# Thirteen quads of block products with seven multiplications in two projections, six shared load buffers, and a later transposition

## The chip, the cores and the metric

The kernel runs on one core of a Trainium2 chip. The metric is device time in microseconds from the start to the end of one execution. TensorE (PE) multiplies matrices: an operand of 128 x 128 is loaded into the array (PEld in the profile) and up to 512 columns run past it; sums go to PSUM, eight banks of 128 x 512 float32. VectorE (DVE) and ScalarE (ACT) work element by element, SyncE (SP) issues most of the DMAs, and GpSimd (POOL) issues some. Each engine carries out its instructions in order.

## The reference

Two layers over 256 positions of width 2048, in float32. The lines that matter here are the two output projections and what stands around them:

```python
# layer A
h = rms_norm(x, a_norm[layer])
q, k, v, g = jnp.split(h @ a_w_in[layer], 4, axis=-1)
o = chunked_relbias_attention(split_heads(q), split_heads(k), split_heads(v), a_rel_bias[layer]).reshape(b, s, D_INNER)
x = x + (o * jax.nn.silu(g)) @ a_w_out[layer]          # projection "ao": 4096 -> 2048
# shared keys and values, forget gates from x; then layer B
q, g = jnp.split(rms_norm(x, b_norm[lb]) @ b_w_in[lb], 2, axis=-1)
o = forgetting_attention(split_heads(q), k_sh, v_sh, cum_logf_h).reshape(b, s, D_INNER)
x = x + (o * jax.nn.silu(g)) @ b_w_out[lb]             # projection "bo": 4096 -> 2048
return rms_norm(x, final_norm)
```

## The kernel before

Every product is a sum of three: each float32 operand is split into a high part `hi` (rounded by ACT) and the rest `lo` (subtracted by DVE), both in the format fp32r, and the products hi·hi, hi·lo and lo·hi are added up in PSUM (`mm3`).

The 256 positions are two tiles, t = 0 and 1. A projection makes four units of 512 columns: `ao0` to `ao3` for layer A, `bo0` to `bo3` for layer B. Each unit has a PSUM bank for each t (`acc`), and its 4096 rows of weights come in 16 sub-blocks, each of two blocks of 128 rows (KB = 2). A sub-block is one load of 512 KB into a buffer `raw`, one split into `hi` (ACT) and `lo` (DVE), and 2 blocks x 2 tiles x 3 = 12 matmuls of 512 columns. `Feed` keeps the loads and splits ahead of the matmuls: `raw` has RAW = 3 buffers, in one ring for all weights of the kernel, `hi` and `lo` have SPLIT = 4 each, and DEPTH = 3 sub-blocks stand ready. A load is issued by SP when the oldest buffer has been read by both splits; SP takes them in program order.

`project` walks through the sub-blocks in the order of a list, unit by unit, and calls two functions: `begun`, which after the unit's twelfth sub-block loads the residual `xin` (in the one buffer "R"), and `closed`, after its last. `ao_closed` adds the two banks to `xin`, writes it to the scratch `x1d`, and starts the turn of the new x, which layer B needs with the width on partitions: for units 0 to 2 that is `x1_to_T`: a STREAM_TRANSPOSE by DVE from `xin` into the one buffer `xinY`, 16 DMAs by POOL from there to `xinZ`, and then splits into `x1Th` and `x1Tl`, in steps some sub-blocks apart (`[8, 1, 1, 1]`). For the last unit it is `x_to_T`, eight transposes on PE ("xT<-ident,xin") at once. Layer B starts with `bqg0`, whose twelve-matmul sub-blocks take their x from these.

`bo_closed` adds the residual, squares it (ACT) and scales it by the last gain; when `bo3` closes, `finish_tile` ends each t with the norm and the output. The last eight sub-blocks of `bo3` (LATE = 8) do t = 0 at once and t = 1 at the end, so that t = 0 can be finished beside the matmuls of t = 1; five of them keep their splits in own tiles (`keep`).

## Time and profile before

| | |
|---|---|
| time, median of 3 runs | 1760.83 us (1760.07 to 1763.58) |
| the profiled execution | 1762.27 us, its span 1760.4 |
| PE busy | 1746.0 us, 99% of the span |
| DVE busy | 1159.1 us, 66% |
| ACT busy | 1084.1 us, 62% |
| POOL busy | 515.7 us, 29% |
| layer A's inputs and attention | 0 to about 711 us |
| projection `ao` | about 711 to 879 us |
| layer B's inputs and attention | about 879 to 1582 us |
| projection `bo` | about 1582 to 1752 us |

The span is the time between the first and last instruction that the profiler saw; the execution's own time is a little longer. A row of the profile names line, engine and operation, the tile that is written and after the arrow those that are read. "Idle before" is the time in which the engine had nothing to do ahead of such an instruction, and after the arrow stands what ended it. Rows of the chain of waits have the start, the duration and the work that the end of the kernel waited for.

### The profile page before, as it was taken

What the parts mean: (1) busy time and instruction counts of PE and PEld (TensorE: products, weight loads), DVE (VectorE), ACT (ScalarE), POOL (GpSimd) and SP (SyncE); (2) the same over time, 40 slices, a digit from 0 to 9 for tenths busy, and PEclk for the clock granted to TensorE, in tenths of its full rate; (3) what the DMA queues carried; (4) which work ended last, traced back from release to release, by engine and by line L of the source; (5) the groups of instructions that cost most, each with busy time, mean ns of one, the idle gap of its engine ahead of it and who ended that gap; (6) DMA issues with size and microseconds to landing.
All of it is one profiled execution on the core that took longest, in us unless ns stands there. A gap on an engine that the chain in (4) does not pass through costs nothing.

```text
span 1760.4 us, 25526 instructions
## 1 busy us (share of the span) xinstructions
PE 1746.0 (99%) x8387; PEld 1533.1 (87%) x8387; DVE 1159.1 (66%) x1662; ACT 1084.1 (62%) x2063; POOL 515.7 (29%) x1071
## 2 busy tenths in 40 slices
PE   9999999999999999999999999999999999999997
PEld 7888888888888888888888888888888888888886
DVE  6666666666666666655666777777777777776654
ACT  6555555555555555555556777777777777765443
POOL 1333333333333333111104333333333333333000
PEclk9999999999999999999999999999999999999999
DMA  7867776777777777777766777777777777776665
GB/s 255 248 218 227 225 225 224 225 224 224 223 224 224 224 225 222 222 239 240 239 195 226 236 227 222 227 224 226 223 228 226 227 222 231 249 225 222 216 217 161
DMA packets 143652, 396.34 MB, mean 225 GB/s; under 512 B 31104, under 2 KB 38560, under 8 KB 143392
## 3 DMA queue, kind: packets, MB, share of 16 engines
q1 hardware_dynamic: 107472, 354.25, 63.8%
q0 software_dynamic: 32256, 37.29, 6.6%
q10 hardware_dynamic: 3792, 3.17, 0.6%
q8 instruction: 66, 1.08, 0.2%
q14 instruction: 66, 0.54, 0.1%
HBM read 351.05 MB, written 4.23 MB: 202 GB/s over the span
## 4 chain that ended last, share of the span: by engine, by line
PE 94%; DMA 2%; DVE 2%; ACT 1%; issue 0%; POOL 0%; SPq 0%; ACTq 0%; DVEq 0%; POOLq 0%
PE bkv_acc L182 19%; PE bqg_acc L182 19%; PE avg_acc L182 18%; PE aqk_acc L182 17%; PE ao_acc L182 9%; PE bo_acc L182 8%; DMA bo_raw<-in_b_w_out 1%; PE op L448 1%; PE s0p L414 1%; PE op L391 0%; PE s1p L390 0%; PE s1p L391 0%; PE op L392 0%; PE op L390 0%; PE s1p L392 0%
## 5 line engine op out<-in xcount | busy, mean ns | idle before, releaser
L363 POOL DMA_DIRECT2D sgZ<-sgY x512 | 250.9, 497 | 194.6 <-DVE sgY L360 96.5
L363 POOL DMA_DIRECT2D turned<-turned x448 | 219.9, 498 | 267.7 <-PE avg_acc L182 93.0
L233 DVE SCALAR_TENSOR_TENSOR bqg_lo<-bqg_raw,gain,bqg_hi 128x512 fp32r<-128x512 f32 x256 | 182.0, 747 | 97.1 <-ACT bqg_hi L232 97.0
L232 ACT ACTIVATE bqg_hi<-bqg_raw,gain 128x512 fp32r<-128x512 f32 x256 | 170.9, 714 | 114.1 <-PE bqg_acc L182 50.2
L238 DVE TENSOR_TENSOR avg_lo<-avg_raw,avg_hi 128x1024 fp32r<-128x1024 f32 x127 | 153.4, 1219 | 115.6 <-ACT avg_hi L237 115.5
L238 DVE TENSOR_TENSOR aqk_lo<-aqk_raw,aqk_hi 128x1024 fp32r<-128x1024 f32 x125 | 152.4, 1219 | 92.7 <-ACT aqk_hi L237 92.6
L233 DVE SCALAR_TENSOR_TENSOR bkv_lo<-bkv_raw,gain,bkv_hi 128x512 fp32r<-128x512 f32 x256 | 181.3, 748 | 45.3 <-ACT bkv_hi L232 42.3
L237 ACT ACTIVATE avg_hi<-avg_raw 128x1024 fp32r<-128x1024 f32 x127 | 132.5, 1055 | 124.5 <-PE aqk_acc L182 60.1
L182 PE MATMUL bqg_acc<-bqg_hi,x1Th 128*128 128x512 f32 x512 | 191.6, 384 | 0.0
L182 PE MATMUL aqk_acc<-aqk_hi,xTh 128*128 128x512 f32 x512 | 190.9, 383 | 0.2
L182 PE MATMUL aqk_acc<-aqk_lo,xTh 128*128 128x512 f32 x512 | 189.0, 379 | 1.2 <-DVE aqk_lo L238 1.2
L182 PE MATMUL avg_acc<-avg_hi,xTh 128*128 128x512 f32 x512 | 190.2, 382 | 0.0
L182 PE MATMUL avg_acc<-avg_lo,xTh 128*128 128x512 f32 x512 | 188.9, 379 | 0.3 <-DVE avg_lo L238 0.3
L182 PE MATMUL bqg_acc<-bqg_hi,x1Tl 128*128 128x512 f32 x512 | 189.1, 379 | 0.0
L182 PE MATMUL bkv_acc<-bkv_hi,x1Th 128*128 128x512 f32 x512 | 189.0, 379 | 0.0
L182 PE MATMUL aqk_acc<-aqk_hi,xTl 128*128 128x512 f32 x512 | 188.9, 379 | 0.0
L182 PE MATMUL avg_acc<-avg_hi,xTl 128*128 128x512 f32 x512 | 188.8, 379 | 0.0
L182 PE MATMUL bkv_acc<-bkv_lo,x1Th 128*128 128x512 f32 x512 | 188.8, 379 | 0.0
L182 PE MATMUL bkv_acc<-bkv_hi,x1Tl 128*128 128x512 f32 x512 | 188.8, 379 | 0.0
L182 PE MATMUL bqg_acc<-bqg_lo,x1Th 128*128 128x512 f32 x512 | 188.8, 379 | 0.0
L237 ACT ACTIVATE aqk_hi<-aqk_raw 128x1024 fp32r<-128x1024 f32 x125 | 131.5, 1052 | 91.9 <-PE avg_acc L182 44.0
L232 ACT ACTIVATE bkv_hi<-bkv_raw,gain 128x512 fp32r<-128x512 f32 x256 | 168.8, 711 | 27.9 <-PE bqg_acc L182 21.4
(205 smaller groups left out, 3442.4 us busy)
## 6 DMA issues: line engine op xcount, KB each, us to landing
bqg_raw<-in_b_w_in SPq DMA_DIRECT2D x128, 512.0 KB, 4.3
bkv_raw<-in_kv_w SPq DMA_DIRECT2D x128, 512.0 KB, 4.0
avg_raw<-in_a_w_in SPq DMA_DIRECT2D x127, 512.0 KB, 4.3
aqk_raw<-in_a_w_in SPq DMA_DIRECT2D x125, 512.0 KB, 3.4
ao_raw<-in_a_w_out SPq DMA_DIRECT2D x64, 512.0 KB, 4.2
bo_raw<-in_b_w_out SPq DMA_DIRECT2D x64, 512.0 KB, 4.2
sgZ<-sgY POOLq DMA_DIRECT2D x512, 40.0 KB, 4.0
turned<-turned POOLq DMA_DIRECT2D x448, 32.0 KB, 3.5
```

Of the source, the lines that this page charges most:

```text
L182: pe.matmul(acc[t], x[:, t * P:(t + 1) * P], w, start=t not in begun, stop=k == nk - 1 and i == 2)
L232: act.activation(hi[:, :, j], raw[:, :, j], AF.Copy, scale=gk)
L233: dve.scalar_tensor_tensor(lo[:, :, j], raw[:, :, j], gk, r32(hi[:, :, j]), op0=OP.mult, op1=OP.subtract)
L237: act.activation(hi[:, :, j], raw[:, :, j], AF.Copy)
L238: dve.tensor_sub(lo[:, :, j], raw[:, :, j], r32(hi[:, :, j]))
L363: queues[j].dma_start(out=r32(z)[j * SQ:(j + 1) * SQ, i], in_=y[i * SQ:(i + 1) * SQ, j])
L414: pe.matmul(s0p[:, i], q0[:, i], qkT[:, HG + i, 0], start=True, stop=True)
L448: pe.matmul(op[:, i, P:], v1[:, i * DH:(i + 1) * DH], pT[:, i, NT], start=False, stop=i == HG - 1)
```

## The change

Three things are changed.

**Quads.** In 13 places two sub-blocks with the same rows of two neighbouring units are done together. They are a 2 x 2 matrix of weight blocks (rows k = 0, 1; units one and two), which stands against the 2 x 2 matrix of x blocks (k = 0, 1; t = 0, 1); in blocks, 8 products of 3 matmuls each. A `Quad` takes the seven products of Winograd's form instead, 21 matmuls for 24. It needs sums of the weight blocks, made by DVE from the loaded buffers (four subtractions of 512 columns: L287, L288, L296, L297), and splits of four sources (`quad_hi0` to `quad_hi3`, `quad_lo0` to `quad_lo3`; the third has 512 columns, the others 1024) instead of two. It needs sums of x blocks as well, made ahead for all the quads of a set by `Quads.open`. Four of the products are summed over the quads of a set in banks `p1`, `p5`, `p7`, `p6`; after the last quad of the set ACT and DVE put them together (`comb`), and each closing adds the result to `xin` (L751 and L924). A set has its place in the list of sub-blocks: 3 quads for `ao0` and `ao1`, 5 for `ao2` and `ao3`, 5 for `bo2` and `bo3`, with three normal sub-blocks behind each but the last, and the rest of the two units behind that. So the first unit of a pair closes just behind the last quad, and the second 6 or 7 sub-blocks later.

**Loads.** RAW is 6, in the one ring. The 12 KB per partition come from a scratch of 4096 bytes for POOL's DMA descriptors (`dynamic_dma_scratch_size`).

**Last transposition.** The eight transposes of `ao3`'s result stand behind the second sub-block of `bqg0`; `B1_STEPS` is taken from the second group on.

The core of the diff:

```diff
-RAW = 3
+RAW = 6
+SCRATCH = 4096
+QUADS = 5
...
         def begin(self, first=None):
             spec, b = next(self.todo, (None, 0))
-            if spec:
+            if isinstance(b, Quad):
+                b.raw = [self.load(u, b.b) for u in b.specs]
+                self.loaded += [(spec, (b, i), b.raw[i - 2] if i > 1 else None, (None, None)) for i in range(4)]
+            elif spec:
...
+            if not spec:
+                self.ready.append(b[0].split(b[1]))
+                self.refill()
+                return
...
         def refill(self):
-            while len(self.loaded) < RAW:
+            while sum(raw is not None for _, _, raw, _ in self.loaded) < RAW:
...
+    class Quad:
+        def split(self, i):
+            one, two = self.raw
+            t = self.all.t[:, 0]
+            if not i:
+                dve.tensor_sub(t[:, :, 0], two[:, :, 0], one[:, :, 0])
+                dve.tensor_sub(t[:, :, 1], two[:, :, 1], two[:, :, 0])
+            src = [one, t, two[:, :, 1:], one][i]
+            n = src.shape[2]
+            hi = stream.tile([P, IL, KB, HN], F32R, name=f"quad_hi{i}", tag="hi", bufs=SPLIT)
+            lo = stream.tile([P, IL, KB, HN], F32R, name=f"quad_lo{i}", tag="lo", bufs=SPLIT)
+            act.activation(hi[:, :, :n], src, AF.Copy)
+            dve.tensor_sub(lo[:, :, :n], src, r32(hi[:, :, :n]))
+            if not i:
+                dve.tensor_sub(one[:, :, 0], two[:, :, 1], t[:, :, 0])
+                dve.tensor_sub(one[:, :, 1], one[:, :, 1], one[:, :, 0])
+            return hi, lo
+        def step(self, lhs, first, second):
...
+            w = feed.get()
+            prod(p1, x(0, 0), w, 0)
+            add(first, 0, x(1, 0), w, 1)
+            w = feed.get()
+            prod(p5, sx(0), w, 0)
+            prod(p7, sx(2), w, 1)
+            w = feed.get()
+            add(second, 0, sx(3), w, 0)
+            w = feed.get()
+            add(first, 1, x(1, 1), w, 1)
+            prod(p6, sx(1), w, 0)
+            if self.last:
+                c = q.comb = q.t.rearrange("p r a j n -> p (r a j n)").rearrange("p (i n) -> p i n", n=UN)
+                act.activation(c[:, 0], p1, AF.Copy)
+                dve.tensor_add(c[:, 3], c[:, 0], p6)
+                dve.tensor_add(c[:, 2], c[:, 3], p5)
+                dve.tensor_add(c[:, 1], c[:, 3], p7)
+                dve.tensor_add(c[:, 3], c[:, 1], p5)
+    class Quads:
+        def order(self, first, second, n, lead):
+            a, b = ([(sp_, i) for i in range(n, sp_["nk"] // KB)] for sp_ in (first, second))
+            normal = a[:-1] + b[:3] + a[-1:] + b[3:]
+            out = normal[:lead]
+            for i in range(n):
+                out.append((None, Quad(self, (first, second), i, not i, i == n - 1)))
+                out += normal[lead + 3 * i:lead + 3 * i + 3] if i < n - 1 else normal[lead + 3 * i:]
+            return out
+        def open(self, lhs, n):
...
+                dve.tensor_add(xs, r32(lhs.hi[k // BIG][:, k % BIG:k % BIG + KB]),
+                               r32(lhs.lo[k // BIG][:, k % BIG:k % BIG + KB]))
+                a11, a21, a12, a22 = (xs[:, j, t * P:(t + 1) * P] for j in range(KB) for t in range(NT))
+                dve.tensor_add(v[:, 0], a21, a22)
+                dve.tensor_sub(v[:, 2], a11, a21)
+                dve.tensor_sub(v[:, 1], v[:, 0], a11)
+                dve.tensor_sub(v[:, 3], a12, v[:, 1])
+                act.activation(hi, v, AF.Copy)
+                dve.tensor_sub(lo, v, r32(hi))
...
+    ao_order = ao_quads.order(ao[0], ao[1], 3, 13) + ao_quads.order(ao[2], ao[3], QUADS, 4)
...
+    bo_order = whole(bo[0]) + whole(bo[1])
     bo_order.insert(KI // KB + WAIT, bo_order.pop(KI // KB - 1))
+    bo_order += bo_quads.order(bo[2], bo[3], QUADS, 4)
...
     def ao_closed(u, acc):
         cs, xin = slice(u * UN, (u + 1) * UN), xins.pop(u)
+        dve.tensor_add(xin, xin, ao_quads.comb[:, u % 2 * NT:u % 2 * NT + NT])
...
-            finish(x_to_T([xin[:, t] for t in range(NT)], u * 4))
+            last.append(x_to_T([xin[:, t] for t in range(NT)], u * 4))
...
-    project(oA, ao_order, ao_begun, ao_closed, [(prev, [2, 6, 2, 1])])
+    project(oA, ao, ao_order, ao_begun, ao_closed, [(prev, [2, 6, 2, 1]), (ao_quads.open(oA, QUADS), [3, 1, 1, 2, 2])])
...
-        accs["qg"] = drive(unit(x1T), prev, B1_STEPS, {}, old, OLD_B_STEPS)
+        accs["qg"] = drive(unit(x1T), prev if g else last[0], B1_STEPS if g else {1: 99}, {}, old, OLD_B_STEPS)
...
+        if u > 1:
+            dve.tensor_add(xin, xin, bo_quads.comb[:, u % 2 * NT:u % 2 * NT + NT])
```

Three places where instructions stand differently. First, DVE around the closing of the second unit of `ao`. Numbers behind a name tell buffers apart. Before:

```order
L626 TENSOR_TENSOR xin<-ao_acc_7142,xin 128x512
L626 TENSOR_TENSOR xin<-ao_acc_7143,xin 128x512
L360 STREAM_TRANSPOSE xinY<-xin 128x1024
L238 TENSOR_TENSOR ao_lo_7484<-ao_raw_7404,ao_hi_7483 128x1024
L238 TENSOR_TENSOR ao_lo_7502<-ao_raw_7422,ao_hi_7501 128x1024
L238 TENSOR_TENSOR ao_lo_7520<-ao_raw_7440,ao_hi_7519 128x1024
L238 TENSOR_TENSOR ao_lo_7538<-ao_raw_7487,ao_hi_7537 128x1024
```

After, with `ao_raw_7428` and `ao_raw_7430` the two loads of the second set's first quad:

```order
L753 TENSOR_TENSOR xin<-ao_acc_7090,xin 128x512
L753 TENSOR_TENSOR xin<-ao_acc_7091,xin 128x512
L248 TENSOR_TENSOR ao_lo_7547<-ao_raw_7410,ao_hi_7546 128x1024
L486 STREAM_TRANSPOSE xinY<-xin 128x1024
L151 TENSOR_TENSOR x1Tl_6780<-xinZ,x1Th_6778 128x128 x2
L294 TENSOR_TENSOR quad_lo_7574<-ao_raw_7428,quad_hi_7573 128x1024
L151 TENSOR_TENSOR x1Tl_6780<-xinZ,x1Th_6778 128x128
L296 TENSOR_TENSOR ao_raw_7428<-ao_raw_7430,ao_quad 128x2x256
L151 TENSOR_TENSOR x1Tl_6780<-xinZ,x1Th_6778 128x128
L297 TENSOR_TENSOR ao_raw_7428<-ao_raw_7428 128x2x256
L294 TENSOR_TENSOR quad_lo_7597<-ao_quad,quad_hi_7596 128x1024
```

The second turn's transpose and the first turn's splits `x1Tl` stand ahead of and among the splits of the first quad, where before a transpose had only `lo` of normal sub-blocks behind it.

Second, DVE within the second set. Before, one `lo` of 1024 columns stands behind the other:

```order
L238 TENSOR_TENSOR ao_lo_7538<-ao_raw_7487,ao_hi_7537 128x1024
L238 TENSOR_TENSOR ao_lo_7556<-ao_raw_7505,ao_hi_7555 128x1024
L238 TENSOR_TENSOR ao_lo_7574<-ao_raw_7523,ao_hi_7573 128x1024
L238 TENSOR_TENSOR ao_lo_7592<-ao_raw_7541,ao_hi_7591 128x1024
L238 TENSOR_TENSOR ao_lo_7610<-ao_raw_7559,ao_hi_7609 128x1024
```

After, from the last split of a quad (its buffers are `ao_raw_7785` and `ao_raw_7787`) to the third split of the next:

```order
L294 TENSOR_TENSOR quad_lo_7964<-ao_raw_7785,quad_hi_7963 128x1024
L287 TENSOR_TENSOR ao_quad<-ao_raw_7903,ao_raw_7901 128x2x256
L248 TENSOR_TENSOR ao_lo_7976<-ao_raw_7868,ao_hi_7975 128x1024
L248 TENSOR_TENSOR ao_lo_7988<-ao_raw_7880,ao_hi_7987 128x1024
L248 TENSOR_TENSOR ao_lo_7997<-ao_raw_7892,ao_hi_7996 128x1024
L288 TENSOR_TENSOR ao_quad<-ao_raw_7903 128x2x256
L294 TENSOR_TENSOR quad_lo_8011<-ao_raw_7901,quad_hi_8010 128x1024
L296 TENSOR_TENSOR ao_raw_7901<-ao_raw_7903,ao_quad 128x2x256
L294 TENSOR_TENSOR quad_lo_8029<-ao_quad,quad_hi_8028 128x1024
L297 TENSOR_TENSOR ao_raw_7901<-ao_raw_7901 128x2x256
L294 TENSOR_TENSOR quad_lo_8045<-ao_raw_7903,quad_hi_8044 128x2x256
```

The first subtraction of the next quad (L287), which needs both of its loads, stands ahead of the three normal `lo` between the quads.

Third, PE at the start of layer B. Before:

```order
L182 MATMUL ao_acc_7821<-ao_hi_8060,oAl_182 128x512
L182 MATMUL bqg_acc_8190<-bqg_hi_8078,x1Th_6772 128x512
L167 MATMUL xT_8142<-ident,xin 128x128
L167 MATMUL xT_8147<-ident,xin 128x128
L182 MATMUL bqg_acc_8191<-bqg_hi_8078,x1Th_6772 128x512
L182 MATMUL bqg_acc_8190<-bqg_hi_8078,x1Tl_6774 128x512
L167 MATMUL xT_8142<-ident,xin 128x128 x3
L167 MATMUL xT_8147<-ident,xin 128x128 x3
```

After (`bqg_hi_8216` is that of the second sub-block, `bqg_hi_8236` of the third):

```order
L184 MATMUL bqg_acc_8312<-bqg_hi_8216,x1Th_6778 128x512
L184 MATMUL bqg_acc_8312<-bqg_lo_8217,x1Th_6778 128x512
L184 MATMUL bqg_acc_8312<-bqg_hi_8216,x1Tl_6780 128x512
L169 MATMUL xT_8353<-ident,xin 128x128 x4
L169 MATMUL xT_8358<-ident,xin 128x128 x4
L184 MATMUL bqg_acc_8311<-bqg_hi_8236,x1Th_6778 128x512
L184 MATMUL bqg_acc_8311<-bqg_lo_8237,x1Th_6778 128x512
L184 MATMUL bqg_acc_8311<-bqg_hi_8236,x1Tl_6780 128x512
```

The eight transposes moved from among the first matmuls of `bqg0` to behind its first 24.

More of the change, by code (lines that the diff above doesn't have):

```diff
@@ L182, in mm3 @@
             pe.matmul(acc[t], x[:, t * P:(t + 1) * P], w,
-                      start=t not in begun, stop=k == nk - 1 and i == 2)
+                      start=t not in begun, stop=last and i == 2)
             begun.add(t)
@@ L265, in get, with __init__, x, sx @@
             return self.ready.pop(0)
+    class Quad:
+        def __init__(self, all_, specs, b, first, last):
+            self.all, self.specs, self.b, self.first, self.last = all_, specs, b, first, last
+        def split(self, i):
[15 more added lines that the diff above has]
+        def step(self, lhs, first, second):
+            q, b = self.all, self.b
+            def x(k, t):
+                return [v(b * KB + k)[:, t * P:(t + 1) * P] for v in (lhs.h, lhs.l)]
+            def sx(i):
+                return q.sums[b][:, 0, i], q.sums[b][:, 1, i]
+            def add(u, t, a, w, j):
+                dot3(u.acc[t], a, [cols(v, j) for v in w], t not in u.begun, not u.left)
+                u.begun.add(t)
+            def prod(p, a, w, j):
+                dot3(p, a, [cols(v, j) for v in w], self.first, self.last)
+            if self.first:
+                q.p = [bank(n) for n in ("p1", "p5", "p7", "p6")]
+            p1, p5, p7, p6 = q.p
+            first.left -= 1
+            second.left -= 1
+            w = feed.get()
[16 more added lines that the diff above has]
+                dve.tensor_add(c[:, 3], c[:, 1], p5)
@@ L313, in step @@
                 self.held.append((b, hi, lo))
+            self.left -= 1
             for j in range(KB):
-                mm3(self.acc, self.lhs, b * KB + j, range(1 if hold else NT), cols(hi, j), cols(lo, j), self.nk,
-                    self.begun)
-            self.left -= 1
+                mm3(self.acc, self.lhs, b * KB + j, range(1 if hold else NT), cols(hi, j), cols(lo, j),
+                    not self.left and j == KB - 1, self.begun)
             if not self.left:
@@ L330, in rest, with project, get @@
             yield u.acc
-    def project(lhs, order, begun, closed, sides):
+    def project(lhs, specs, order, begun, closed, sides):
         units = {}
+        def get(u):
+            if u not in units:
+                units[u] = Unit(lhs, specs[u])
+            return units[u]
         for sp_, b in order:
-            u = int(sp_["name"][-1])
-            if u not in units:
-                units[u] = Unit(lhs, sp_)
-            units[u].step(b)
-            begun(u, b)
+            if sp_:
+                us = [int(sp_["name"][-1])]
+                get(us[0]).step(b)
+            else:
+                us = [int(u["name"][-1]) for u in b.specs]
+                b.step(lhs, *(get(u) for u in us))
+            for u in us:
+                begun(u, units[u].left)
             for side, steps in sides:
@@ L347, in project @@
                         steps.pop(0)
-            if not units[u].left:
-                more = closed(u, units[u].acc)
-                if more:
-                    sides.append(more)
+            for u in us:
+                if not units[u].left:
+                    more = closed(u, units[u].acc)
+                    if more:
+                        sides.append(more)
         for side, _ in sides:
@@ L611, in x1_to_T @@
             yield
-    xins = {}
+    xins, last = {}, []
     def load_xin(src, u):
```

46 lines of the change are left out of this document (29 added, 17 removed).

## The prediction

> **What bounds the kernel now.** I read the page's first part, then the busy time by stage (span; busy us of PE, PEld, DVE, ACT and POOL with their instructions; granted clock, DMA share, GB/s), then the chain of waits, to see what a matmul less is worth.
>
> ```profile
> PE 1746.0 (99%) x8387; PEld 1533.1 (87%) x8387; DVE 1159.1 (66%) x1662; ACT 1084.1 (62%) x2063; POOL 515.7 (29%) x1071
> 740.00:960.00 220.00, 219.89 (x1047) 192.56 (x1047) 134.07 (x198) 121.36 (x212) 37.34 (x76) 1.00 0.70 225
> 1600.00:1760.00 160.00, 151.06 (x708) 131.88 (x706) 85.56 (x97) 71.03 (x93) 7.83 (x16) 0.98 0.64 204
> 738.91 139.86 PE ao_acc L182 x648
> ```
>
> TensorE (PE) is the bound nearly everywhere: in the stage with the first projection it idles 0.11 of 220 us, in the last stage 8.9 of 160, nearly all of it behind the last matmul. VectorE (DVE) has some 40% of room in both. The chain row gives the price of a matmul: 139.86 / 648 = 0.2158 us. A sub-block (12 matmuls) is 2.59 us, a quad (21) 4.53, and a quad with its three sub-blocks 57 matmuls = 12.30, where 60 took 12.95.
>
> **What is removed.** 13 quads leave out 3 matmuls each: 39 x 0.2158 = **-8.4 us**, all of it on the bound. Two waits of before go too:
>
> ```profile
> 878.78 0.22 PE bqg_acc L182
> 880.60 19.43 PE bqg_acc L182 x90
> PE bo_acc L182 <- DVE bo_lo L238: 0.8, 1, 0.8
> ```
>
> From 878.78 to 880.60 three weight matmuls (0.65) stand beside eight transposes: 1.17 more than the matmuls alone. The eight transposes stay; some 0.6 of the 1.17 is waiting, which goes: **-0.6**. The wait for `bo_lo` at 1739 is that of three load buffers, which six remove: **-0.8**. The list of PE's waits names no other that a deeper lookahead would end, so loading further ahead gains nothing elsewhere. The transposes that are moved issue no DMA.
>
> **What is added, and whether DVE hides it.** The groups of the first projection by line (count, busy us, mean ns, idle before), the landing times of `ao_raw`, and a load of the tail in the chain of waits:
>
> ```profile
> L238 DVE TENSOR_TENSOR ao_lo<-ao_raw,ao_hi 128x1024 fp32r<-128x1024 f32 x61 | 74.5, 1222 | 65.1 <-ACT ao_hi L237 64.8
> L626 DVE TENSOR_TENSOR xin<-ao_acc,xin 128x512 f32<-128x512 f32 x8 | 5.1, 682 | 0.0
> L149 DVE TENSOR_TENSOR x1Tl<-xinZ,x1Th 128x128 fp32r<-128x128 f32 x24 | 5.8, 284 | 0.0
> L237 ACT ACTIVATE ao_hi<-ao_raw 128x1024 fp32r<-128x1024 f32 x61 | 64.4, 1055 | 72.1 <-PE ao_acc L182 48.3 <-DMA ao_raw<-in_a_w_out 23.8
> DMA to landing us min/median/max: 3.1/4.2/7.4
> 1720.19 3.58 DMA bo_raw<-in_b_w_out
> ```
>
> A quad and its three sub-blocks ask DVE for four block subtractions of 512 columns (0.69 each), three splits of 1024 and one of 512, and three `lo` of 1024: 4 x 0.69 + 6 x 1.22 + 0.69 = 10.8 of 12.30 us. By sum that is hidden; by order it is not quite. The first subtraction (L287) of the next quad stands ahead of the three `lo` of the sub-blocks and waits for both of that quad's loads. The second load is the seventh of six buffers, so SP issues it only when this quad's third split (`quad_lo` of 512) is done. From L287 to that split DVE works 9.1 us (three `lo`, four subtractions, two splits of 1024, one of 512; back to back they overlap a little). The loop is therefore 9.1 + landing against 12.30: no wait if the load lands in under 3.2, and what it takes above that is a wait at every quad. The `ao_raw` row bounds the landing at 3.1 and (median) 4.2; the load of the tail that went out alone took 3.58. Here the late load is nearly alone as well, the others having gone out 4 us earlier: I take 3.4, near the lone one, so 0.23 a link (0 to 1.0). Two links in the first set: **+0.5** (0 to 2.0); two in the second: **+0.5** (0 to 2.0). In the last projection three, and between its fourth and fifth quad the last split of the one stands behind the subtraction of the other, by about the load and a subtraction less what PE has in hand, 1.2 us: **+1.9** (0 to 4.3).
>
> The new closing adds and the sums of x (DVE 128-column rows, 0.28, and 512, 0.69) lie ahead of the quads beside full matmuls, at no cost: DVE idles 65 us over the 61 `ao_lo`. Without that cover a set of five sums would cost about 5 x (2 x 0.69 + 4 x 0.28) = 12.5 us.
>
> **Start of the second set of quads.** Here an order of before is no longer harmless. After `ao1` closes its residual is turned by a STREAM_TRANSPOSE into the one buffer xinY, from which 16 POOL DMAs of the turn before still read. The first such turn in the trace, in order of time, and the landing times of `xinZ`:
>
> ```profile
> 755.45 1.25 DVE L360 STREAM_TRANSPOSE xinY<-xin 128x1024 f32<-128x1024 f32 x1
> 757.32 4.41 POOL L363 DMA_DIRECT2D xinZ<-xinY  x9 [18.23 <-PE ao_acc L182]
> 766.27 0.99 POOL L363 DMA_DIRECT2D xinZ<-xinY  x2 [0.63 <-DMA xinZ<-xinY]
> DMA to landing us min/median/max: 2.8/4.5/5.7
> ```
>
> The turn is over 756.70 to 767.26 + 4.5 = 15.1 us after its transpose (13.4 to 16.3). Before, two turns stood 41 us apart; now `ao1` closes seven sub-blocks behind `ao0`. From the start of the first set's last quad (T = 0): the quad ends at 4.53; the closing adds come between `lo` 12 to 15, of which the last waits for buffers that PE frees at 12.30, then takes 1.06 on ACT and 1.22 on DVE; the transpose ends at 15.8, its DMAs have landed at 30.9. PE wants the next quad at 4.53 + 11 x 2.59 = 33.0. But on DVE the second transpose (till 32.2) and two splits of x1T (0.28 each) stand ahead of the quad's first split, which ends at 34.0, the second at 37.1 and the fourth at 40.1, with two subtractions and six x1T splits between them. The quad ends at 41.4, for 37.6. Then L287 of the next quad, whose load goes out behind the third split (38.35), ends at 42.5 and `lo` 9 at 43.8: PE goes on at 43.8 where 37.6 was due, **+6.2** (4.5 with the shortest landings, 7.4 with the longest), in pieces of 1 to 2.4 us. SP, in its turn, stands at the load of `xin` for `ao1` till the write of `ao0`'s residual has landed; the weight loads behind it are those of sub-blocks six and more ahead, which the six buffers cover.
>
> **First projection into layer B.** The eight transposes of the last residual now stand behind two sub-blocks of `bqg0`. The DMA list has the write of the residual (median us at its end); the landing row is that of `xin`:
>
> ```profile
> x1d<-xin SPq DMA_DIRECT2D x8, 256.0 KB, 4.2
> DMA to landing us min/median/max: 4.0/5.0/6.6
> ```
>
> From the last quad's end: `ao2` closes on DVE at 8.7, between `lo` 13 to 15; its x1d write must land (4.2) before the last `xin` is loaded into the same buffer (5.0, 4.0 to 6.6): 18.2. Then come an add of 1024 (1.22), a `lo` (0.75), and two adds of 0.68: 22.7 with the handovers. PE is there after 6 + 2 sub-blocks, at 20.7: **+2.0** (1.0 to 3.6). The turned third residual lands at about 26, which PE wants at 28.
>
> **Tail.** The DMA list and the timeline of the last stage:
>
> ```profile
> xin<-x1d SPq DMA_DIRECT2D x4, 512.0 KB, 5.0
> 1741.51 0.69 DVE L762 TENSOR_TENSOR xin<-bo_acc,xin 128x512 f32<-128x512 f32 x1 [1.44 <-PE bo_acc L182]
> 1742.98 1.28 ACT L778 ACT_TABLE_LOAD   x1
> 1745.24 0.88 DVE L787 TENSOR_SCALAR xg<-xg,fin 128x512 f32<-128x512 f32 x2
> 1751.87 0.69 DVE L762 TENSOR_TENSOR xin<-bo_acc,xin 128x512 f32<-128x512 f32 x1 [5.75 <-PE bo_acc L182]
> ```
>
> Before, the first half (t = 0) of `bo3` was finished from 1741.51 to 1746.1 (4.6 us with the table load), ten us ahead of the second. Now `bo2` closes about 8 us after the last quad, and only then can the last `xin` be loaded (5.0); with one more add of 1024 (1.22) t = 0 starts some 14 us after that quad, and PE ends at 15.5. The 4.6 us then lie in front of t = 1, on the same engines: 14.2 + 4.6 = 18.8 against 15.9, up to 3 late; if the loads of the last sub-blocks keep PE as well, it is less: **+1.2** (0 to 3.2).
>
> **Sum.** -8.4 - 0.6 - 0.8 + 0.5 + 6.2 + 0.5 + 1.9 + 2.0 + 1.2 = +2.5 us. The profiled execution took 1762.27 (span 1760.4), 1.4 above the median of the runs, 1760.83; the change against its own time is carried over: **1763.3 us**, +0.14%. This measurement can tell about 0.2% from no change (3.5 us: 1757.3 to 1764.4).
>
> **Rivals.**
>
> 1. The cover holds, on the other side: the loads land in 3.2 us or less (3.1 is the row's minimum), the links cost nothing, and the turn lands early enough or DVE catches up. With the lower bounds of every term but the turn's (4.5) and the boundary's (1.0) the sum is -9.8 + 5.5 = -4.3: 1756.5; with those gone too 1751.0. For it speaks DVE's room; against it that the turn's 15 us rest on POOL's row and 11 sub-blocks are not enough. It decides whether the second transposition leaves DVE before T = 30. Chance 0.28.
>
> 2. Landing like the median, 4.2 and more: the links cost 1.0 each and 1.7 at the fourth quad; in all 2.0 + 2.0 + 4.3, with 6.2, 2.0 and 1.2 as above: +7.9, 1768.7. For it speaks the median, against it that in before most loads queue behind another one. Chance 0.22.
>
> 3. POOL's copies get slower, as their scratch shrinks to 4096 bytes. POOL is 29% busy, so the layers would hide it, but the turn would not: if its 16 issues went at the pace of the last ones (two in 1.8 us, from 764.51 to 766.27), they take 14 us for 10, and the second set starts 4 later: about 1767. The trace of before can't show it. Chance 0.04. [...]
>
> 4. The pauses at the second set bring the granted clock down. The stage rows have it at 1.00 with pauses of 0.8 us, and the last at 0.98, where PE idles at the end. If half the clock were granted for 3.4 us after each of two pauses, 3.4 us more come: about 1767. My pieces stay under 2.5 us, so chance 0.04. [...]
>
> **The numbers.** The forecast has 0.42, from 1759.5 to 1767 (0.33 below 1764.4, 0.09 above). Faster: rival 1, 0.28. Same: 0.33. Slower: 0.09 + 0.22 + 0.04 + 0.04 = 0.39. The range reaches from rival 1's 1753 (its lowest end left out, 0.1) to 1769.5 (0.1 above).
>
> **What would show it.** Right: in the changed profile x39 fewer 128x512 matmuls; PE idle between the two sets of quads, 4 to 7 us in the stretch of `quad_lo` behind a second STREAM_TRANSPOSE; waits of PE for `quad_lo` and `lo` of 0.2 to 1 us at each quad; xT waiting for xin at the start of B by 1 to 3; the last `xin` loaded under 5 us before the last matmul. Wrong: if PE stays at 99.9% through both projections (then it is rival 1), if POOL's DMA rows are longer than 498 ns, or a granted clock under 1.00.

## The result and the profile after

The changed kernel takes 1764.53 us (median of 17 runs, 1761.86 to 1770.13), the kernel before in the same session 1761.25 (17 runs, 1759.75 to 1764.56). The ratio is 1.0018, with a 95% interval of 1.0010 to 1.0026: 3.3 us more, which is little, but the interval leaves out no change. 2.5 us more were forecast. The profiled execution of the changed kernel took 1764.38 (span 1762.7). Its busy times, in the page's first part:

```profile
PE 1741.2 (99%) x8348; PEld 1531.0 (87%) x8348; DVE 1244.9 (71%) x1818; ACT 1108.3 (63%) x2102; POOL 516.8 (29%) x1071
```

TensorE runs 8387 - 8348 = 39 matmuls fewer, as counted, and is busy 4.8 us less, not 8.4, in part because some of those left ran at half the clock (below). VectorE has 86 us more to do. PE's list of waits (us in total, times, longest) names the places:

```profile
PE xT L169 <- DVE xin L753: 2.9, 2, 2.7
PE op L516 <- ACT wideh L508: 2.6, 2, 2.2
PE ao_acc L184 <- DVE ao_lo L248: 2.2, 1, 2.2
...
PE bo_acc L517 <- DVE quad_lo L294: 0.9, 1, 0.9
PE ao_acc L517 <- DVE quad_lo L294: 0.3, 1, 0.3
PE p L517 <- DVE quad_lo L294: 0.3, 1, 0.3
```

The wait for `bo_lo` is gone, and these six rows are new or longer. (A wait is counted where an engine had nothing to do; the row of `op` adds up two places, one of them in the first 100 us.) By stage, cut at the first matmul of each projection in the timeline of PE (us; the kernels of the experiments are explained below):

| kernel | to first `ao` | `ao` | layer B | `bo`, to its last matmul | after it | span |
|---|---|---|---|---|---|---|
| before | 711.6 | 167.0 | 702.8 | 170.1 | 9.0 | 1760.4 |
| after | 710.3 | 167.2 | 708.8 | 167.0 | 9.4 | 1762.7 |
| e1, before with six load buffers | 710.1 | 167.0 | 702.8 | 169.0 | 9.0 | 1757.8 |
| e7, quads in `bo` only | 710.7 | 167.0 | 705.6 | 167.2 | 9.3 | 1759.8 |
| e4, after, last residual loaded at once | 710.0 | 167.4 | 704.5 | 166.9 | 9.4 | 1758.1 |

The first projection leaves out 24 matmuls (5.2 us) and is no shorter. The last leaves out 15 (3.2) and is 3.1 shorter. Layer B, in which nothing was to be saved, is 6.0 longer.

**The first projection.** VectorE around the start of the second set of quads in the changed kernel, in order of time (start, us, the instruction, and in brackets its idle time and what ended it):

```profile
785.29 1.25 DVE L486 STREAM_TRANSPOSE xinY<-xin 128x1024 f32<-128x1024 f32 x1
793.82 1.23 DVE L751 TENSOR_TENSOR xin<-xin,ao_quad 128x1024 f32<-128x1024 f32 x1 [1.05 <-DMA xin<-in_x]
799.28 1.25 DVE L486 STREAM_TRANSPOSE xinY<-xin 128x1024 f32<-128x1024 f32 x1 [1.71 <-DMA xinZ<-xinY]
800.82 1.22 DVE L294 TENSOR_TENSOR quad_lo<-ao_raw,quad_hi 128x1024 fp32r<-128x1024 f32 x1
809.31 0.69 DVE L287 TENSOR_TENSOR ao_quad<-ao_raw,ao_raw 128x512 f32<-128x512 f32 x1 [1.98 <-DMA ao_raw<-in_a_w_out]
```

This is the chain of the forecast: the second transposition waits (1.71) for the copies of the first, and the quad's splits stand behind it; then the next quad's subtraction (L287) waits 1.98 for a load that went out late. PE, of the same stretch, and then the granted clock in three windows of 3.41 us (window, its length, PE busy with its matmuls, clock, DMA share, GB/s):

```profile
804.84 0.48 PE L517 MATMUL p<-quad_lo,ao_sums 128*128 128x512 f32 x1 [0.29 <-DVE quad_lo L294]
807.38 0.48 PE L517 MATMUL ao_acc<-quad_lo,oAh 128*128 128x512 f32 x1 [0.34 <-DVE quad_lo L294]
811.19 0.48 PE L184 MATMUL ao_acc<-ao_lo,oAh 128*128 128x512 f32 x1 [2.24 <-DVE ao_lo L248]
```

```profile
808.79:812.20 3.41, 1.17 (x6) 1.00 0.80 244
812.20:815.62 3.42, 3.42 (x10) 0.52 0.79 277
815.62:819.03 3.41, 3.41 (x17) 0.98 0.64 239
```

Behind the longest pause there, 2.24, the clock is at half for one window: 10 matmuls where the next has 17. The chain of waits has the three sub-blocks from there on as one piece, beside the next three (one matmul's record is missing in the first):

```profile
811.19 9.51 PE ao_acc L184 x35
825.23 7.77 PE ao_acc L184 x36
```

9.51 - 7.77 = 1.7 us is the price of the clock. The stage as a whole gives the sum: 167.0 - 24 x 0.2158 = 161.8 were due, 167.2 came, so the start of the second set costs 5.3, of which 1.7 is the clock and 3.6 are pauses (2.87 of idle time, and what the matmuls around each pause lose).

**Layer B.** PE at the transposes and in the last attention, then VectorE ahead of that, in the changed kernel and, last two rows, in the kernel before:

```profile
885.58 0.30 PE L169 MATMUL xT<-ident,xin 128*128 128x128 f32 x1 [2.72 <-DVE xin L753]
1547.10 0.39 PE L516 MATMUL op<-wideh,vh 128*128 128x256 f32 x1 [2.20 <-ACT wideh L508]
```

```profile
1513.95 0.42 DVE L509 TENSOR_TENSOR widel<-turned,wideh 128x256 fp32r<-128x256 f32 x1 [4.25 <-ACT wideh L508]
1526.71 0.69 DVE L370 TENSOR_TENSOR bo_quad<-oBh,oBl 128x512 f32<-128x512 f32 x1
1528.63 1.50 DVE L486 STREAM_TRANSPOSE sgY<-sg 128x1280 f32<-128x1280 f32 x1
```

```profile
1510.25 0.43 DVE L383 TENSOR_TENSOR widel<-turned,wideh 128x256 fp32r<-128x256 f32 x1 [2.48 <-ACT wideh L382]
1522.35 1.51 DVE L360 STREAM_TRANSPOSE sgY<-sg 128x1280 f32<-128x1280 f32 x1
```

At the transposes the gap between two weight matmuls is 4.13 us (882.48 to 886.83 less a matmul), where before had 1.17 with its transposes: 3.0 more. The second wait was in no step of the forecast. The same matmul `op` stood at 1542.81 before without a wait: 4.3 later, and 1.9 of that (the start's -1.1 and the boundary's +3.0) was already there, so 2.4 more are lost. The matmuls of `op` behind the pause start further apart and lose another 0.6: from the last weight matmul ahead of `op` to the first behind it are 4.24 us (1544.52 to 1548.76), where before had 1.29. So the two places, 3.0 each, are the whole of the 6.0. The last transposition of `sg` stands 6.3 later on VectorE than before, behind sums of x for the quads of `bo` (L370 and the lines after it). Of this, 1.9 is PE's own lateness; 2.6 come between the split of the turned queries (`widel`) and the transposition, 14.68 us for 12.10, where the sums lie; and the remaining 1.8 were there when the turned queries landed.

**Tail.** The last wait of `bo` and the last matmul:

```profile
1724.41 0.48 PE L517 MATMUL bo_acc<-quad_lo,oBh 128*128 128x512 f32 x1 [0.89 <-DVE quad_lo L294]
1753.22 0.38 PE L184 MATMUL bo_acc<-bo_hi,oBl 128*128 128x512 f32 x1
```

One link between quads waits, from the fourth to the fifth of `bo`, 0.89. From the last matmul's start to the end of the span are 9.4, about 0.5 more than before: as forecast, the last scaling of t = 0 (VectorE, 1752.91, 0.89 long) lies just ahead of the add for t = 1 (1753.71).

### The profile page after: what moved, and what is told of

It is laid out like the page before. It is cut to its first block, busy times and chain, and to the rows that moved or that the text cites. A ratio compares the mean times of both kernels' runs of the same rounds, so it can differ in the third digit from the quotient of the medians.

```text
span 1762.7 us, 25633 instructions
## 1 busy us (share of the span) xinstructions
PE 1741.2 (99%) x8348; PEld 1531.0 (87%) x8348; DVE 1244.9 (71%) x1818; ACT 1108.3 (63%) x2102; POOL 516.8 (29%) x1071
## 4 chain that ended last, share of the span: by engine, by line
PE 93%; DVE 3%; DMA 2%; issue 1%; ACT 1%; POOL 0%; ACTq 0%; SPq 0%; DVEq 0%; POOLq 0%
PE aqk_acc L184 19%; PE bkv_acc L184 19%; PE avg_acc L184 19%; PE bqg_acc L184 18%; PE bo_acc L184 6%; PE ao_acc L184 5%; PE op L574 1%; PE s0p L540 1%; DVE quad_lo L294 0%; DMA xinZ<-xinY 0%; PE op L517 0%; PE s1p L517 0%; PE s1p L516 0%; PE s1p L518 0%; PE op L518 0%
## 5 line engine op out<-in xcount | busy, mean ns | idle before, releaser
L242 ACT ACTIVATE bkv_hi<-bkv_raw,gain 128x512 fp32r<-128x512 f32 x256 | 168.7, 712 | 22.9 <-PE bqg_acc L184 16.7
```

The source lines that it names most:

```text
L242: act.activation(hi[:, :, j], raw[:, :, j], AF.Copy, scale=gk)
```

## The experiments

Each ratio is to the kernel before, run on the same chip in the same session (its medians 1761.4 to 1761.6), with a 95% interval. Differences to the changed kernel are of medians from different sessions, between which that of before moved by 0.3. The theory at the outset was the forecast's: the second set starts late because of the first turn's copies, the boundary because of the late load of the last residual. Rivals: the smaller scratch of POOL's copies, one cause other than the turn, and the links of the loop.

### What each part is worth

**e1: the load buffers and the scratch alone, on the kernel before.**

```diff
-RAW = 3
+RAW = 6
-nc = bacc.Bacc("TRN2", target_bir_lowering=False, num_devices=1)
+nc = bacc.Bacc("TRN2", target_bir_lowering=False, num_devices=1, dynamic_dma_scratch_size=4096)
```

> The kernel before with six load buffers and the smaller descriptor scratch alone; no quads, transposes where they were. If deeper loading only takes away waits, as the forecast has it, the wait of 0.8 us for bo_lo in the last stage goes and some of the 1.5 us of waits in the first 45 us: 1 to 2 us faster than before, 1759 to 1760. If the smaller scratch or the deeper queue of weight loads holds up POOL's copies (the rival), PE waits for wideh more often, 2 us each as at 1547 us in the changed kernel, POOL's landing median rises over 4.0 us, and the time is 1761 to 1764.

Measured: 1759.79 (1758.96 to 1760.75), 0.9988 [0.9979, 0.9997]. As expected: the wait for `bo_lo` is gone and the first projection starts 1.5 earlier. One sign of the other reading did come: `sgZ` lands in 4.3 us (median; 4.0 before). But no wait of PE for the turned copies is added, and the time is lower, so the smaller scratch costs nothing that shows in the time (rival 3). This part alone makes a kernel that is faster by 0.12%, and it is the best of all that were run. Against it, not against before, the quads and the moved transposes cost 4.7 us.

**e7: quads in the last projection only**, the first as before, its transposes too.

```diff
-ao_order = ao_quads.order(ao[0], ao[1], 3, 13) + ao_quads.order(ao[2], ao[3], QUADS, 4)
+ao_order = [i for sp_ in ao for i in whole(sp_)]
...
-last.append(x_to_T([xin[:, t] for t in range(NT)], u * 4))
+finish(x_to_T([xin[:, t] for t in range(NT)], u * 4))
```

> The changed kernel with the quads of layer B's projection alone: the units of layer A one after the other without quads, its transposes at its end as before. Six buffers and the small scratch stay. Against the run with six buffers alone (1759.8): 15 matmuls less, 3.2 us, against one pause of 0.9 us at the fifth quad and an end 0.5 us later: 1.5 to 2 us faster than that, 1757.5 to 1758.5. If the quads' DVE work costs more than the pause shows (rival), no faster than 1759.8.

Measured: 1760.47 (1758.25 to 1763.78), 0.9991 [0.9983, 1.0000], 2 to 3 us above what was expected. In its profile `bo` is 1.8 shorter than in e1, the end 0.4 longer, and layer B 2.8 longer. PE's waits, of which the longest under `op` stands at 1544:

```profile
PE op L516 <- ACT wideh L508: 2.1, 2, 1.1
...
PE bo_acc L517 <- DVE quad_lo L294: 1.1, 1, 1.1
```

So the quads of `bo` alone bring the wait in the last attention. From the weight matmul ahead of `op` to the one behind it are 3.16 us, 1.29 in e1: 1.9 lost, as much as `bo` saves. Another 1.0 of layer B, most of it ahead of the last attention, is not assigned.

**e4: the last residual gets a buffer of its own.** `xin` of the fourth unit of `ao` lies in a buffer that is free by then, so its load need not wait until the write to `x1d` has landed.

```diff
+if u == 3 and src is xf:
+    xins[u] = home[1].rearrange("p j n u -> p (j n u)").rearrange("p (t n) -> p t n", t=NT)
+else:
     xins[u] = att.tile([P, NT, UN], F32, name="xin", tag="R")
```

> The changed kernel with the last residual of layer A loaded into that free tile instead of the one buffer R, so its load doesn't wait for the write of the one before. If that wait is what holds up the moved transposes, PE's wait for xT (2.9 us) falls to under 0.3: 2.5 to 3 us faster than the changed kernel, about 1762. If DVE's queue holds them up (rival: a transposition of 1.25 and the splits of bqg0 stand ahead), 1.5 us or more of the wait remain.

Measured: 1761.08 (1758.58 to 1764.46), 0.9994 [0.9986, 1.0003], 3.5 under the changed kernel. Its list of PE's waits begins

```profile
PE ao_acc L184 <- DVE ao_lo L248: 2.3, 1, 2.3
PE op L516 <- ACT wideh L508: 1.6, 2, 1.3
```

and has no `xT` row: the boundary's cost was that load. The wait of the second set is as long as in the changed kernel, and the clock is at half once behind it, as there (0.89 over 800 to 815 us, 0.91 in the changed kernel).

**e9: the transposes back at the end of `ao`.**

```diff
-last.append(x_to_T([xin[:, t] for t in range(NT)], u * 4))
+finish(x_to_T([xin[:, t] for t in range(NT)], u * 4))
...
-accs["qg"] = drive(unit(x1T), prev if g else last[0], B1_STEPS if g else {1: 99}, {}, old, OLD_B_STEPS)
+accs["qg"] = drive(unit(x1T), prev, B1_STEPS, {}, old, OLD_B_STEPS)
```

> The changed kernel with the eight transposes back at the end of layer A's projection. The last residual is ready at 885 us while PE gets there at 878: if that is so, PE waits some 7 us for 3, and the clock is halved once more: 4 to 6 us slower than the changed kernel, 1768.5 to 1771. If the late residual is itself a consequence of the later place (rival: the planner puts its adds further back), the wait stays near 3 us and the time near 1764.5.

Measured: 1767.08 (1763.73 to 1769.34), 1.0027 [1.0018, 1.0037]: 2.5 above the changed kernel. The wait grows from 2.72 to 4.39, and the clock is at half once more behind it (0.91 over 880 to 900 us, 1.00 in the changed kernel):

```profile
886.91 0.41 PE L169 MATMUL xT<-ident,xin 128*128 128x128 f32 x2 [4.39 <-DVE xin L753]
```

So the moved transposes are worth 2.5 us here; with quads the residual is later than they can follow, even moved.

**e10: four load buffers.**

```diff
-RAW = 6
+RAW = 4
```

> The changed kernel with four load buffers for six. A quad holds two, and the two of the next are then the fifth and, with three sub-blocks between, the tenth of the ring: if the landing of the second load is what DVE waits for, every quad waits one more landing, 2 to 4 us at 13 quads: 1785 to 1815, with pauses before each quad. If the splits that stand ready cover it (rival), under 1768.

Measured: 1776.53 (four runs, 1774.93 to 1777.31), 1.0079 [1.0065, 1.0093]. Less than was expected, since not every quad waits, but PE waits at five splits where it waited at one, and at the transposes for longer:

```profile
PE xT L169 <- DVE xin L753: 5.2, 1, 5.2
PE p L517 <- DVE quad_lo L294: 4.9, 5, 1.6
```

With six buffers the loop from a quad's split over its load to the next quad is covered; with four it is not. Not all of the 12 us more are waits: the mean granted clock in this profile was 0.994, in the changed kernel's 0.998, which over the two spans comes to an estimated 6 us.

### What holds up the start of the second set

**e3: the second turn gets buffers of its own**, so that its transposition need not wait for the first turn's copies.

```diff
-z = turn(xin.rearrange("p t (c d) -> p (t c) d", d=P), NT * 4, "xin")
+z = turn(xin.rearrange("p t (c d) -> p (t c) d", d=P), NT * 4, "xin", home=home if u == 1 else None)
```

> The changed kernel with the second turn in the tile of the attention's turns, which is free there, instead of xinY and xinZ. The transpose then waits for no DMA of the first turn. If that wait is what costs at the second set, the first quad's splits come about 1 us earlier, the pauses there fall from 3.4 us to 1.5 or less, and the clock isn't halved (1.7 us more): 1.5 to 3.5 us faster than the changed kernel, 1761 to 1763. If the late load of the second quad is the whole of it (rival), the pause ahead of ao_lo stays at 2.2 and the clock drops as before: within 1 us of the changed kernel.

Measured: 1764.95 (1760.35 to 1769.66), 1.0016 [1.0007, 1.0026]: nothing gained. VectorE in its profile:

```profile
795.62 1.23 DVE L751 TENSOR_TENSOR xin<-xin,ao_quad 128x1024 f32<-128x1024 f32 x1 [2.23 <-DMA xin<-in_x]
799.28 1.24 DVE L486 STREAM_TRANSPOSE turned<-xin 128x1024 f32<-128x1024 f32 x1
809.86 0.69 DVE L287 TENSOR_TENSOR ao_quad<-ao_raw,ao_raw 128x512 f32<-128x512 f32 x1 [2.08 <-DMA ao_raw<-in_a_w_out]
```

The transposition no longer waits for the copies and still stands at 799.28, where it was: the closing add (L751) now waits 2.23 for the residual's load, which itself waits for the write of the residual before. Two waits end together, and the forecast had named one. `ao` takes 167.1 us in this profile.

**e12: both removed**, the second residual loaded into a buffer of its own as well.

```diff
+own = [home[0], att.tile([P, NQ, NT * 4, SQ], F32, name="xinZ", tag="Z")] if u == 1 else None
+z = turn(xin.rearrange("p t (c d) -> p (t c) d", d=P), NT * 4, "xin", home=own)
...
+if u % 2 and src is xf:
+    xins[u] = home[1].rearrange("p j n u -> p (j n u)").rearrange("p (t n) -> p t n", t=NT)
```

> The changed kernel with the second and fourth residual of layer A loaded into the free tile of the attention's turns, and the second turn's transpose written into its other half, so that DVE waits ahead of the second set neither for that load nor for the first turn's DMAs. What is left is the first turn's splits, which stand ahead of the first quad's and can't begin before the first turn has landed (29.4 us after the last quad began). If that third wait ends at the same moment as the two others, the pauses at the second set stay over 2 us and the clock is halved as before: 1760 to 1762, as with the last residual moved alone. If the two waits were the cause: 1756 to 1757.5.

Measured: 1761.66 (1759.12 to 1763.40), 0.9999 [0.9990, 1.0008]: not faster than e4, and within the 1760 to 1762 that were expected if a third wait ends at the same moment. The quad's splits now wait for splits of the first turn ahead of them, and the load is late again:

```profile
809.65 0.69 DVE L287 TENSOR_TENSOR ao_quad<-ao_raw,ao_raw 128x512 f32<-128x512 f32 x1 [1.73 <-DMA ao_raw<-in_a_w_out]
811.53 0.48 PE L184 MATMUL ao_acc<-ao_lo,oAh 128*128 128x512 f32 x1 [1.99 <-DVE ao_lo L248]
```

In its profile the clock stays up (1.00 from 800 to 825), and `ao` still takes 167.4.

**e11: the splits of the first turn moved behind the quad too.**

```diff
 # on top of e12
-return more and (more, [8, 1, 1, 1])
+return more and (more, [8 if u else 11, 1, 1, 1])
```

> The same, and the first turn's splits three items later in the list (11 for 8), behind the first quad's. All three waits on the first turn are then off DVE's queue ahead of the second set: no pause over 0.5 us there, no halved clock, no wait for xT: about 1761.1 - 3.4 - 1.7 = 1756, and under the kernel before (1761.5) by 0.2 to 0.4%. If the late load of the second quad alone makes the pause (rival), L287 still waits 2 us for it and the time is 1760 or more.

Measured: 1761.44 (1757.39 to 1765.45), 0.9996 [0.9986, 1.0005], where 1756 was expected if these were the three causes. The pause shrinks and does not go, and at each of the two links that the profile shows here the second half of the next quad comes late:

```profile
806.52 0.69 DVE L287 TENSOR_TENSOR ao_quad<-ao_raw,ao_raw 128x512 f32<-128x512 f32 x1 [1.91 <-DMA ao_raw<-in_a_w_out]
808.41 0.48 PE L184 MATMUL ao_acc<-ao_lo,oAh 128*128 128x512 f32 x1 [1.39 <-DVE ao_lo L248]
```

```profile
847.07 0.69 DVE L287 TENSOR_TENSOR ao_quad<-ao_raw,ao_raw 128x512 f32<-128x512 f32 x1 [1.58 <-DMA ao_raw<-in_a_w_out]
848.95 0.48 PE L184 MATMUL ao_acc<-ao_lo,oAh 128*128 128x512 f32 x1 [1.19 <-DVE ao_lo L248]
```

`ao` takes 167.1 us in this profile: in e3, e12 and e11 a wait of VectorE ahead of the second set was taken out each time, and in none is the projection shorter than the 167.2 of the changed kernel by more than 0.2. Elsewhere this execution lost something too, in the last attention, where the clock fell behind a wait of 2.34:

```profile
1543.73:1547.15 3.42, 3.40 (x13) 0.50 0.29 68
```

The windows from 770 to 800 us show how VectorE's room shrinks (PE, PEld, DVE, ACT, POOL busy, then the clock). Before, after, and e11:

```profile
770.00:800.00 30.00, 30.00 (x140) 26.27 (x140) 18.39 (x24) 16.76 (x28) 1.33 (x3) 1.00 0.67 205
```

```profile
770.00:800.00 30.00, 30.00 (x141) 26.33 (x140) 24.27 (x26) 17.52 (x27) 7.87 (x16) 1.00 0.85 285
```

```profile
770.00:800.00 30.00, 30.00 (x141) 26.27 (x140) 28.15 (x30) 17.32 (x24) 7.89 (x16) 1.00 0.86 291
```

VectorE has 11.6 of 30 us free before, 5.7 after, and 1.9 in e11, where splits of the second set have moved into the stretch. That it has no room left there to get ahead of PE is a reading of these rows, and not shown. What e11 shows is its rival: L287 still waits about 2 us. The load that it waits for went out at 801.10, as soon as the third split was done (801.07), and landed in 5.31 us (L287 starts at 806.52), where such a load between settled quads of the changed kernel took 3.1 to 3.2.

### Attempts to make the quads pay

**e6: e3 and e4 together, and the fourth residual of `bo` in a buffer of its own.**

```diff
+z = turn(xin.rearrange("p t (c d) -> p (t c) d", d=P), NT * 4, "xin", home=home if u == 1 else None)
+if u == 3:
+    xins[u] = home[1].rearrange("p j n u -> p (j n u)").rearrange("p (t n) -> p t n", t=NT)
```

> Both edits, and the last residual of layer B in that tile too, so that its first half is finished early. If the three waits add up: pauses 3.4 to under 1.5, no halved clock, xT wait gone, and the end 0.5 us closer to the last matmul: 5 to 7 us faster than the changed kernel, 1757.5 to 1759.5, under the kernel before. If they hide each other or another wait comes in their place (DVE is 88% asked for between quads): 1761 or more.

Measured: 1764.86 (1760.20 to 1769.97), 1.0019 [1.0009, 1.0030]: missed by 5 us and more. The second set pauses as in e3, and the last projection has two waits that no other kernel here shows, 0.71 for ScalarE's half of `bo_keep` and then

```profile
1737.34 0.48 PE L184 MATMUL bo_acc<-bo_keep,oBh 128*128 128x512 f32 x1 [1.04 <-DVE bo_keep L248]
```

Why the early residual of `bo` brings these stays open.

**e8: e4 with four quads in the second set, after six sub-blocks instead of four.**

```diff
 # on top of e4
-ao_quads.order(ao[2], ao[3], QUADS, 4)
+ao_quads.order(ao[2], ao[3], 4, 6)
...
-(ao_quads.open(oA, QUADS), [3, 1, 1, 2, 2])
+(ao_quads.open(oA, 4), [3, 1, 1, 2, 2])
```

> The changed kernel with the last residual of layer A in the free tile, and in the second set of layer A four quads for five, begun six sub-blocks after the first pair closes instead of four. If the start of that set is only too early for the first turn, which lands at about 29 us after the last quad begins, the three pauses there (3.4 us with the slots lost) and the halved clock (1.7 us) go, for 3 matmuls more (0.65 us): 4 to 5 us faster than with the residual moved alone (1761.1), 1756 to 1757. If the second quad's late load makes the pause whatever comes ahead (rival), the clock record still has a half and the time is about 1761.

Measured: 1763.01 (1760.93 to 1766.90), 1.0006 [0.9997, 1.0015], for the 1756 to 1757 expected of the theory that the quads only come too soon. The pauses are 0.29, 2.64 and 1.99, and `ao` takes 169.1. SyncE's queue and VectorE:

```profile
803.98 0.38 SPq L746 DMA_DIRECT2D xin<-in_x  x1
805.49 30.65 SPq L206 DMA_DIRECT2D ao_raw<-in_a_w_out  x12
```

```profile
816.77 0.69 DVE L287 TENSOR_TENSOR ao_quad<-ao_raw,ao_raw 128x512 f32<-128x512 f32 x1 [2.58 <-DMA ao_raw<-in_a_w_out]
```

The weight loads (12 of them from 805.49) now stand behind the load of `xin`, which goes out only at 803.98, when its buffer is free. The later start moved the quads against another place of the same queue.

**e13: e4 with three quads there, after ten sub-blocks.**

```diff
 # on top of e4
-ao_quads.order(ao[2], ao[3], QUADS, 4)
+ao_quads.order(ao[2], ao[3], 3, 10)
...
-(ao_quads.open(oA, QUADS), [3, 1, 1, 2, 2])
+(ao_quads.open(oA, 3), [3, 1, 1, 2, 2])
```

> The changed kernel with the last residual of layer A in the free tile, and in the second set of layer A three quads for five, begun ten sub-blocks after the first pair closes instead of four; the waits for the first turn and for the second residual stay as they are. If what costs at the second set is that DVE has too little room there (closings, transposes and splits of the turn on top of 10.8 of 12.3 us for a quad and its sub-blocks), so that any wait of DVE reaches PE, then no pause is left there and the clock isn't halved: 1761.1 - 3.4 - 1.7 + 6 x 0.2158 = 1757.3, under the six buffers alone (1759.8) and the kernel before (1761.5). If the load of a quad's second half is late by itself (rival), pauses of 1 to 2 us stay at the quads of that set: 1759.5 or more.

Measured: 1764.62 (1762.93 to 1768.20), 1.0020 [1.0011, 1.0029], far from 1757.3, which was expected if a lack of room on VectorE were the cause, as there is more room with fewer quads and a later start. `ao` takes 169.9, 2.7 more than in the changed kernel, for 6 matmuls more (1.3); the clock is at half once, from about 824.1, where seven matmuls take 0.63 us for the 0.38 of those before. Now the splits of the second turn stand in the first quad, and VectorE waits with them for its copies:

```profile
820.09 0.29 DVE L151 TENSOR_TENSOR x1Tl<-xinZ,x1Th 128x128 fp32r<-128x128 f32 x1 [5.44 <-ACT x1Th L150]
```

```profile
821.26 0.48 PE L516 MATMUL p<-quad_hi,ao_sums 128*128 128x512 f32 x1 [1.44 <-ACT quad_hi L293]
```

**e14: e13 with four quads in `bo`, after six sub-blocks.**

```diff
 # on top of e13
-bo_order += bo_quads.order(bo[2], bo[3], QUADS, 4)
+bo_order += bo_quads.order(bo[2], bo[3], 4, 6)
...
-(bo_quads.open(oB, QUADS), [20, 2, 2, 2, 2])
+(bo_quads.open(oB, 4), [20, 2, 2, 2, 2])
```

> The same, and in layer B's projection four quads for five, begun after six sub-blocks for four, so that the first unit of the pair closes nine sub-blocks before the end for six. If the pause of 0.9 us at the fifth quad and the end that is 0.5 us later come from that closing's being late, both go, for 3 matmuls more (0.65): 0.5 to 1 us faster than the run above, 1756.5. If the last eight sub-blocks of the last unit hold the end (rival), no faster, 1757.5 to 1758.5.

Measured: 1764.74 (1761.61 to 1767.12), 1.0017 [1.0008, 1.0026]. The wait of the last attention is gone. That this comes of one set of sums less is not shown: e3 and e10, with all five, have no wait there either, and from `widel` to the transposition of `sg` are 14.68 us here as in all the others. The link before the last quad still pauses 0.92.

## Why the prediction was right, and where it was not

The size came out (2.5 us forecast, 2.3 in the span, 3.3 between the medians), and in part that was luck: the links, the tail and the second set cost 3.6 less than forecast and the start gained 1.3 that was not forecast, while the boundary cost 1.6 more and the last attention 3.0 that the sum did not have. By its steps:

| step | forecast | profile |
|---|---|---|
| 39 matmuls less | -8.4 | -8.4 by count |
| wait for `bo_lo` | -0.8 | -0.8 |
| transposes: waits beside them gone, boundary late | -0.6 + 2.0 | +3.0 |
| links of the loop | +0.5 + 0.5 + 1.9 | +0.9 |
| start of the second set | +6.2 | +3.6 in pauses, +1.7 by the clock |
| tail | +1.2 | +0.5 |
| start of the first projection | none | -1.3 |
| last attention of layer B | none | +3.0 |
| sum | +2.5 | about +2.2 |

Of the four signs that the prediction gave for being right, one came as it stood, the wait of `xT` (1 to 3; 2.9). The idle time between the two sets was 2.87 for 4 to 7, only some quads had a wait, and the last `xin` went out 9.5 us before the last matmul, not under 5. And a granted clock under 1.00, one of its signs of being wrong, was seen.

**The second set.** The mechanism held. From the start of the first set's last quad (769.8), the first transposition ends at 16.7 (forecast 15.8), the second at 30.7 (32.2), the quad is due and starts at 33.1 (33.0). The pauses were over-sized, 6.2 for 3.6, because the first turn's copies landed 12.6 us after its transposition and not 15.1, and the splits went in about 1.5 us earlier: inside the quad 1.1 were lost for the 3.8 worked out, behind it 2.4 as forecast. What failed in the reasoning is the single cause: "it decides whether the second transposition leaves DVE before T = 30" names the turn's copies, and e3 shows that without them the residual's load gives the same time. Behind these stand the first turn's splits (e12) and the second load (e11), and with all of them out of the way the projection is still as long. Which step would free the start stays open. Two readings are left, a lack of room on VectorE and a second load that lands late by itself. e11 came out on the side of the second; in e13 more room brought no gain, but there a new wait stands in the way. No run tested either alone.

**The clock.** Rival 4 had a chance of 0.04 and wanted two pauses of which each costs 1.7; one came, and the half clock for 3.4 us that it took for each is what followed (0.52 over 3.42 us). "My pieces stay under 2.5 us" was right (2.24) and did not protect. That a pause has to be longer than that to bring the clock down was the author's assumption, which no run shows; one of 2.24 us was enough. Nor did the rows that it cited bear on this: the one pause of 0.8 us lies in the row with 0.98.

**The links** were forecast too dear, and the term at fault is the landing of the late load. 3.4 us were taken for it, and the prediction's own bound for no wait was 3.2. Between settled quads it landed in 3.1 to 3.2 (the loads issued at 756.65, 844.35, 1694.36 and 1706.71), as rival 1 had it, and the loop on VectorE took 8.9 us for 9.1 (847.62 to 856.52), so L287 waits for no load there. The loop is seen only where a quad comes late (at 809.31, and before the last quad of `bo`). e10 shows that it is real: with two buffers less PE waits at five splits.

**The boundary** had the right cause, shown by e4 (no wait, 3.5 us faster) and e9 (2.5 slower without the move). The forecast was +1.4 for both its terms together; the wait alone is 2.9.

**The start.** "Loading further ahead gains nothing elsewhere" did not hold: the first projection starts 1.3 earlier, 1.5 in e1. A wait of 1.9 for `wideh` in the first 100 us of before is 0.4 in the changed kernel and 0.2 in e1. Eleven of the twelve profiles with six buffers start the projection at 709.6 to 711.1, before at 711.6 (e8, at 712.6, ran at 0.51 of the clock from 84.06 to 87.47). There is one profile of before, so how much of this the buffers bring is not shown.

**The missed step** is "The new closing adds and the sums of x ... lie ahead of the quads beside full matmuls, at no cost". Their sum is hidden; their place is not. Those of `bo` stand on VectorE in layer B's last attention, ahead of the transposition that PE's `op` waits for some 18 us later. Of the twelve kernels with quads in `bo` nine have a wait there of 0.4 to 2.3 us, three have none, and neither before nor e1 has one; e7, where `bo` alone has quads, has it. That the sums cause it was read from the order on VectorE; no run moved them alone. The numbers fit: in all twelve the way from `widel` to the transposition takes 2.58 us longer than in before and e1, and no wait in the last attention is longer than that. In the three without a wait the way is as long; the copies ahead of it and behind it land sooner or later from kernel to kernel, and with them the wait comes or not.

No version with quads beat e1: the best, e7, e4 and e11, lie within 0.1% of the kernel before.

## What to carry to other kernels

Room on average is not room in order. With the quads VectorE still had 20% of the first projection free, and 19% of the 30 us ahead of the second set, and their splits came late all the same, each behind an instruction that waited. Added work on an engine off the bound also has a place: look at what stands behind it, even a stage earlier, as with the sums of x in layer B's attention. When a wait is on a queue that runs in order, list every instruction ahead of the late one, since removing the last releaser only shows the next. And test the small enabling part by itself: the six load buffers, with the smaller scratch that makes room for them, were the whole gain.

## What was not expected of the hardware

The granted clock fell to half behind a pause of 2.24 us. In the changed kernel PE was busy for 1.17 us from 808.79 to 812.20, and behind that the trace has a record of half the clock, 3.413 us long from 812.34 on. A longer pause, 2.72 us at 882.86, left the clock where it was:

```profile
880.46:883.88 3.42, 2.40 (x12) 1.00 0.97 343
883.88:887.29 3.41, 1.50 (x10) 1.00 0.56 147
```

In e3 the longest wait at the same place was much the same, 2.8 us, and the clock fell: PE was busy for 1.10 us from 884.13 to 887.55, and from there to 890.96 the clock was 0.52. In e12 a wait of 1.99 left it at 1.00 (800 to 825 us). In e8 PE was busy for 1.75 us from 80.65 to 84.06, in small matmuls, and had 0.51 of the clock from there to 87.47. So in these profiles the length of a pause did not tell whether the clock would fall, and what brings it down is not shown. In the changed kernel the pause of 2.24 us cost itself and 1.7 us more, the one of 2.72 only itself. This may add to the spread of the runs (8.3 us between the ends of 17, against 4.8 before), but their granted clocks, 0.995 to 0.999, do not put them in the order of their times.
